# Issuing the second halves of the first six input tiles from ScalarE's DMA queue in a one-core hybrid decoder step

## The chip, the cores and the metric

One core of one Trainium2 chip runs the whole kernel. The metric is the device time of one execution in microseconds (us). Three runs of the kernel before gave 923.28, 923.93 and 924.47 us; their median is 923.93 us.

## What is computed

One layer of a decoder trunk over 1024 prompt rows and 8 sample rows (1032 rows, 1024 channels, float32). The start of it is what matters here:

```
h = rmsnorm(x, norm_g) * (1 + scale(c)) + shift(c)      # scale, shift, gate from silu(c) @ w_ada
p = h @ w_in                                            # twelve slices feed three branches
v = layernorm(gelu(p[b_v]))                             # the slice that is computed first
...                                                     # three branches, merge by sigmoid gates
x = x + gate(c) * (merged @ w_out);  y = rmsnorm(x, final_g)
```

The RMS norm needs the sum of squares over all 1024 channels of a row, so all of x has to be on the chip before any product of h can begin.

## The kernel before, in words

x lies transposed: eight tiles of 128 channels by 1032 rows. Each tile is loaded in two halves of 512 rows (256 KB each), x0 to x7 with halves a (`hf` 0) and b (`hf` 1); the eight sample columns come by a small DMA of their own (`xsm`, L342) and GpSimd copies them in (L156). The tiles go in the order 0, 4, 1, 5, 2, 6, 3, 7 (`ORDER`, L42).

Every engine works off its own list of instructions in the order of the program. SyncE (SP) issues all DMAs of the kernel before: `pk` (L105), `xsm` (L342), the sixteen halves of x (L155), and then by turns a tile of the v weights (`bvr`, L172) and two of the modulation weights (`ada`, L161). The framework gives every DMA one of eight completion counters in turn, in the order of the program; a DMA is issued only once the earlier one on its counter has landed. Counted from `pk`, the eighteenth DMA, x7b, so waits for the tenth, x5b.

ScalarE's list begins with a table load and a one-element activation (L127), the SiLU of the conditioning (L128, which waits for `pk`), a second table load and a one-element activation (L129). Then `sum_squares` (L189 to L206) follows: one Square per tile in the order of the tiles (L195, each waits for both halves of its tile), and for the last tile two Squares of half the width (L200). VectorE adds the squares up: five adds over whole tiles (L197) and four over halves (L203, L204). TensorE, which runs 110 dummy matmuls meanwhile (`warm_up`, L286, no input from x), forms the row sums from the added squares (L184). After it come the reciprocal root (L212 to L217), its spreading over the partitions (L226), the modulation product (`ada_mm`, L267) with its transposes (L275), the scaling of x (L241, L251), the split of h into two parts (L255, L259) and the first v products (L337 to L339). The rest of the kernel, over 800 us of it, is a row of matmul jobs that the change does not touch.

The order of the load around the change:

```
    Q.dma_start(xsm, ins["xT2"])
    for k in ORDER:
        load_x(k)
    for i in range(3):
        load_wbv(i)
        ada[i] = load_ada(ORDER[i])
    ss = sum_squares()
```

`Q` is SyncE, `A_` ScalarE, `G_` GpSimd, `V` VectorE.

Of the kernel before, what the change touches and what calls it, by code (L numbers as in the profile page):

```python
# [33 lines left out]
HP, HS = SEQ // 2, NS // 2  # L34
H = HP + HS
# [6 lines left out]
ORDER = (0, 4, 1, 5, 2, 6, 3, 7)  # L42
# [4 lines left out]
OC = ((128, 388, 4), (644, 388, 4), (0, 256, 2))  # L47
OE = 128
WIN = (2, 4, 8, 16)


def f32(ap):
# [4 lines left out]
def hybrid_step_kernel(ctx: ExitStack, tc: tile.TileContext, ins, outs):  # L57
# [8 lines left out]
    def S(name, cols=SLOT, dt=F32, rows=P):  # L66
        return sp.tile([rows, cols], dt, tag="T", name=name)
# [10 lines left out]
    def samples(ap):  # L78

        return halves(ap)[:, :, HP:H]  # L80
# [7 lines left out]
    V, A_, G_, PE, Q = nc.vector, nc.scalar, nc.gpsimd, nc.tensor, nc.sync  # L88
# [57 lines left out]
    xh = {}  # L146
# [5 lines left out]
    def load_x(k):  # L152
        xh[k] = S(f"x{k}", T)
        for hf in range(2):
            Q.dma_start(xh[k][:, H * hf : H * hf + HP], ins[f"xT{hf}"][:, k, :])  # L155
        G_.tensor_copy(samples(xh[k]), xsm[:, k, :].rearrange("p (h t) -> p h t", h=2))  # L156

    def load_ada(k):
# [184 lines left out]
    for k in ORDER:  # L343
        load_x(k)
# [34 lines left out]
    for i in range(KD):  # L379
        k = ORDER[i]  # L380
# [461 lines left out]
    def c_pair(g, n):  # L842
        st = {}
        w = WIN[g]

# [474 lines left out]
```

## Time and profile before

| | us |
|---|---|
| median of three runs | 923.93 |
| the profiled execution, device time | 925.24 |
| its span, first to last instruction | 923.5 |
| TensorE busy | 903.7 |
| ScalarE busy | 354.8 |
| VectorE busy | 563.0 |
| last half of x landed, first Square of the last tile | 17.48 |
| first row sum on TensorE | 18.99 |

The profile is one execution under the hardware profiler. The span is counted from the first to the last instruction, and 1.74 us of the device time lie outside it. Times in the rows are us from the span's start. An engine's name with a q behind it (SPq, ACTq) is that engine's sequencer, which issues DMAs and waits on semaphores. The granted clock is the share of TensorE's full clock: 1.00 is 2.4 GHz and 0.50 is 1.2 GHz.

### The profile page before, as it was taken

To read this page: it belongs to the slowest core of one execution; us is meant where nothing else is said; L and a number is where in the kernel's file an instruction comes from. 1 tells how busy PE (TensorE), PEld (TensorE's weight loads), DVE (VectorE), ACT (ScalarE), POOL (GpSimd) and SP (SyncE) were. 2 spreads that over 40 slices of the span, in tenths; PEclk is the share of its full clock that TensorE was granted. 3 is DMA by queue.
4 is the path that set the end of the run, shared out by engine and by line. 5 is a ranking of instruction groups with operands and counts; after the bars stand their busy time and mean duration, and the time that the engine had idled before them with its cause. 6 is when DMAs were issued, how large, how long until landed. Compare 5 with 4: busy or idle time off the path is not lost.

```text
span 923.5 us, 16546 instructions
## 1 busy us (share of the span) xinstructions
PE 903.7 (98%) x6910; PEld 874.1 (95%) x6910; DVE 563.0 (61%) x1016; ACT 354.8 (38%) x639; POOL 37.5 (4%) x76
## 2 busy tenths in 40 slices
PE   7998999999999999999999999999999999999995
PEld 7666999999999999999999999999999899999994
DVE  4686757656666576656465566574454466583634
ACT  5565473454342333335343454444422301431211
POOL 1354000000000000000000000000000000000001
PEclk8899999999999999999999999999999999999997
DMA  9904222212321212123304205132579834170103
GB/s 322 384 6 116 79 93 68 82 47 106 101 92 47 69 47 69 47 82 121 132 1 160 94 12 190 52 124 96 207 297 343 300 137 183 50 225 1 61 10 115
DMA packets 50058, 110.15 MB, mean 119 GB/s; under 512 B 10552, under 2 KB 21560, under 8 KB 49984
## 3 DMA queue, kind: packets, MB, share of 16 engines
q1 hardware_dynamic: 49984, 109.10, 34.0%
q8 instruction: 54, 0.88, 0.4%
q14 instruction: 20, 0.16, 0.1%
HBM read 85.24 MB, written 23.84 MB: 118 GB/s over the span
## 4 chain that ended last, share of the span: by engine, by line
PE 91%; POOL 2%; DVE 2%; DMA 1%; issue 1%; ACT 1%; SPq 0%; DVEq 0%; POOLq 0%; ACTq 0%
PE o L1077 3%; PE o L1078 3%; PE o L1079 3%; PE g_2B L525 2%; PE g_0B L525 2%; PE g_3B L528 2%; PE g_3B L525 2%; PE g_2B L527 2%; PE g_2B L528 2%; PE g_0B L527 2%; PE g_3B L527 2%; PE g_1B L528 2%; PE g_1B L525 2%; PE g_0B L528 2%; PE g_1B L527 2%; DMA x<-in_xT 1%
## 5 line engine op out<-in xcount | busy, mean ns | idle before, releaser
L1077 PE MATMUL o<-mh,woh 128*128 128x388 f32 (+1 forms) x192 | 62.2, 324 | 0.0
L1078 PE MATMUL o<-ml,woh 128*128 128x388 f32 (+1 forms) x192 | 61.4, 320 | 0.0
L1079 PE MATMUL o<-mh,wol 128*128 128x388 f32 (+1 forms) x192 | 61.3, 319 | 0.0
L1077 PEld LDWEIGHTS o<-mh,woh 128*128 128x128 f32 x192 | 36.1, 188 | 0.3
L1078 PEld LDWEIGHTS o<-ml,woh 128*128 128x128 f32 x192 | 36.1, 188 | 0.3
L1079 PEld LDWEIGHTS o<-mh,wol 128*128 128x128 f32 x192 | 36.1, 188 | 0.0
L1180 ACT ACTIVATE osq<-xr 128x388 f32<-128x388 f32 (+1 forms) x21 | 10.3, 491 | 48.4 <-DVE xr L1169 28.0
L337 PE MATMUL v<-bvw,hhi 128*128 128x512 f32 x64 | 27.2, 425 | 1.6 <-ACT v L613 1.1
L339 PE MATMUL v<-bvw,hlo 128*128 128x512 f32 x64 | 25.8, 403 | 1.1 <-DVE hlo L259 0.8
L91 ACT ACTIVATE mh<-acc 128x516 fp32r<-128x516 f32 (+1 forms) x14 | 9.2, 690 | 44.4 <-DVE acc L979 40.7
L338 PE MATMUL v<-bvw,hhi 128*128 128x512 f32 x64 | 25.5, 398 | 0.0
L1166 DVE SCALAR_TENSOR_TENSOR xr<-o,gt,xr 128x384 f32<-128x384 f32 x16 | 9.8, 614 | 18.5 <-PE o L1079 18.5
L525 PE MATMUL g_2B<-t,g_2w 128*128 128x258 f32 x72 | 20.4, 284 | 0.0
L528 PE MATMUL g_3B<-hhi,g_3wB 128*128 128x258 f32 x72 | 20.4, 283 | 0.0
L525 PE MATMUL g_0B<-t,g_0w 128*128 128x258 f32 x72 | 20.4, 283 | 0.0
L528 PE MATMUL g_1B<-hhi,g_1wB 128*128 128x258 f32 x72 | 20.4, 283 | 0.0
L337 PEld LDWEIGHTS v<-bvw,hhi 128*128 128x128 f32 x64 | 12.3, 192 | 8.6 <-issue 3.3
L528 PE MATMUL g_2B<-hhi,g_2wB 128*128 128x258 f32 x72 | 20.3, 283 | 0.0
L527 PE MATMUL g_0B<-hlo,g_0wB 128*128 128x258 f32 x72 | 20.3, 282 | 0.0
L527 PE MATMUL g_2B<-hlo,g_2wB 128*128 128x258 f32 x72 | 20.3, 282 | 0.0
L525 PE MATMUL g_3B<-t,g_3w 128*128 128x258 f32 x72 | 20.3, 282 | 0.0
L528 PE MATMUL g_1B<-t,g_1w 128*128 128x258 f32 x72 | 20.3, 282 | 0.0
(1043 smaller groups left out, 3490.7 us busy)
## 6 DMA issues: line engine op xcount, KB each, us to landing
sig<-sd SPq DMA_DIRECT2D x24, 516.0 KB, 5.9
ada<-in_ada SPq DMA_DIRECT2D x18, 512.0 KB, 8.6
yr<-yd SPq DMA_DIRECT2D x12, 516.0 KB, 10.2
x<-in_xT SPq DMA_DIRECT2D x16, 256.0 KB, 5.9
gr<-in_ada_g SPq DMA_DIRECT2D x8, 512.0 KB, 10.4
wor<-in_wo SPq DMA_DIRECT2D x8, 512.0 KB, 5.4
xr<-in_xf SPq DMA_DIRECT2D x8, 512.0 KB, 3.9
sd<-g_0o SPq DMA_DIRECT2D x6, 516.0 KB, 3.3
```

What stands on the lines that cost most here:

```text
L91: A_.activation(hi, src, AF.Copy)
L337: PE.matmul(vacc[i], lhsT=lh, rhs=w[:, 0, :], start=start, stop=False)
L338: PE.matmul(vacc[i], lhsT=lh, rhs=w[:, 1, :], start=False, stop=False)
L339: PE.matmul(vacc[i], lhsT=ll, rhs=w[:, 0, :], start=False, stop=stop)
L525: PE.matmul(o, lhsT=w[:, 0, f_], rhs=bh, start=start and k == 0, stop=False, skip_group_check=True)
L527: PE.matmul(o, lhsT=w[:, 0, f_], rhs=bl, start=False, stop=False, skip_group_check=True)
L528: PE.matmul(o, lhsT=w[:, 1, f_], rhs=bh, start=False, stop=stop and k == KW - 1, skip_group_check=True)
L1077: PE.matmul(o, lhsT=wo_h[k][:, w], rhs=cols(mhi[k]), start=start, stop=False)
L1078: PE.matmul(o, lhsT=wo_h[k][:, w], rhs=cols(mlo[k]), start=False, stop=False)
L1079: PE.matmul(o, lhsT=wo_l[k][:, w], rhs=cols(mhi[k]), start=False, stop=stop)
L1166: V.scalar_tensor_tensor(x[:, :m], ps[:, :m], gt[:, f, 0:1], x[:, :m], ALU.mult, ALU.add)
L1180: A_.activation(o_like(c, sq), x, AF.Square)
```

## The change

The half b of the tiles 0, 4, 1, 5, 2 and 6 is issued by ScalarE into its own DMA queue. The half a of these tiles, and both halves of tiles 3 and 7, stay with SyncE. Nothing else differs; the DMAs keep their order in the program, and so their completion counters.

```diff
+XQ = 6
...
     def load_x(k):
         xh[k] = S(f"x{k}", T)
         for hf in range(2):
-            Q.dma_start(xh[k][:, H * hf : H * hf + HP], ins[f"xT{hf}"][:, k, :])
+            q = A_ if hf and k in ORDER[:XQ] else Q
+            q.dma_start(xh[k][:, H * hf : H * hf + HP], ins[f"xT{hf}"][:, k, :])
         G_.tensor_copy(samples(xh[k]), xsm[:, k, :].rearrange("p (h t) -> p h t", h=2))
```

In the order of the program the DMAs are: pk, xsm, x0a, x0b*, x4a, x4b*, x1a, x1b*, x5a, x5b*, x2a, x2b*, x6a, x6b*, x3a, x3b, x7a, x7b, and then the weights; a star marks those that ScalarE issues now. In ScalarE's list the six stand behind the activation of L129 and ahead of the first Square.

## Rows read from the trace of the kernel before

**Rows 1.** The page's table of busy time: engine, us, share of the span, instructions.

```profile
PE 903.7 (98%) x6910; PEld 874.1 (95%) x6910; DVE 563.0 (61%) x1016; ACT 354.8 (38%) x639; POOL 37.5 (4%) x76
```

**Rows 2.** The chain that ended last, from the start to the first v products: start us, us, what held it.

```profile
1.72 0.42 SPq L155
...
4.56 0.43 SPq L155
...
5.04 6.39 DMA x<-in_xT
...
11.44 5.96 DMA x<-in_xT
...
17.48 0.64 ACT sq L200
...
18.15 0.71 DVE sq L204
...
18.99 3.65 PE ss L184 x24
22.64 1.86 PE pada L267 x16
```

**Rows 3.** The timeline of ScalarE from L128 to the last Square: start us, us, engine, line, operation, out<-in, count, and in brackets the idle time before it and what ended it.

```profile
2.75 0.27 ACT L128 ACTIVATE sc<-pk 128x72 f32<-128x72 f32 x1 [0.46 <-DMA pk<-in_pk]
3.04 1.28 ACT L129 ACT_TABLE_LOAD   x1
4.33 0.20 ACT L129 ACTIVATE warm<-ones 128x1 f32<-128x1 f32 x1
5.46 1.06 ACT L195 ACTIVATE sq<-x 128x1032 f32<-128x1032 f32 x1 [0.92 <-DMA x<-in_xT]
8.84 1.06 ACT L195 ACTIVATE sq<-x 128x1032 f32<-128x1032 f32 x1 [2.32 <-DMA x<-in_xT]
10.18 1.06 ACT L195 ACTIVATE sq<-x 128x1032 f32<-128x1032 f32 x1 [0.28 <-DMA x<-in_xT]
11.53 1.06 ACT L195 ACTIVATE sq<-x 128x1032 f32<-128x1032 f32 x1 [0.28 <-DMA x<-in_xT]
12.85 1.06 ACT L195 ACTIVATE sq<-x 128x1032 f32<-128x1032 f32 x1 [0.25 <-DMA x<-in_xT]
14.16 1.07 ACT L195 ACTIVATE sq<-x 128x1032 f32<-128x1032 f32 x1 [0.25 <-DMA x<-in_xT]
15.51 1.06 ACT L195 ACTIVATE sq<-x 128x1032 f32<-128x1032 f32 x1 [0.28 <-DMA x<-in_xT]
17.48 1.16 ACT L200 ACTIVATE sq<-x 128x516 f32<-128x516 f32 x2 [0.92 <-DMA x<-in_xT]
```

**Rows 4.** Busy time by stretch: us from the start, then the stretch's length, busy us (instructions) of PE, PEld, DVE, ACT and POOL, the granted clock, the mean busy share of the 16 DMA engines, and GB/s.

```profile
2.50:3.50 1.00, 1.00 (x7) 1.00 (x6) 0.17 (x1) 0.74 (x2) 0.30 (x3) 1.00 0.70 163
3.50:5.50 2.00, 2.00 (x14) 2.00 (x14) 0.00 (x0) 1.06 (x3) 0.76 (x7) 1.00 0.99 354
5.50:9.00 3.50, 3.50 (x34) 3.50 (x33) 0.00 (x0) 1.18 (x2) 0.00 (x0) 1.00 0.89 228
9.00:15.50 6.50, 6.41 (x58) 6.21 (x56) 5.13 (x5) 5.16 (x5) 0.00 (x0) 1.00 1.05 396
15.50:18.40 2.90, 0.00 (x0) 0.00 (x0) 1.98 (x3) 1.98 (x3) 0.00 (x0) 1.00 1.04 410
18.80:32.00 13.20, 13.01 (x70) 8.88 (x71) 8.56 (x25) 5.39 (x13) 1.66 (x6) 0.50 1.03 411
```

**Rows 5.** What ScalarE's sequencer carried out for L128: line, engine, operation, count, duration ns min/median/max, first and last start us.

```profile
L128 ACTq EVENT_SEMAPHORE  x1: 17/17/17, 2.7 to 2.7; - x1
```

**Rows 6.** A later stretch of ScalarE: its timeline, and ahead of it the one instruction that its sequencer carried out for L303 between 58.5 and 60 us (the columns as in rows 5 and 3).

```profile
L303 ACTq EVENT_SEMAPHORE  x1: 17/17/17, 59.0 to 59.0; - x1
...
58.83 1.07 ACT L255 ACTIVATE hhi<-x 128x1032 fp32r<-128x1032 f32 x1 [0.56 <-POOL x L253]
59.80 0.37 ACT L270 ACTIVATE adap<-pada 128x256 f32<-128x256 f32 x1
60.07 0.62 ACT L177 ACTIVATE bvw<-bvr 128x512 fp32r<-128x512 f32 x1
62.62 0.64 ACT L303 ACTIVATE t<-x 128x516 fp32r<-128x516 f32 x1 [1.93 <-POOL x L299]
```

**Rows 7.** DMAs by the stretch in which they were issued (3.1 to 3.5, 3.5 to 4.05, 12.1 to 12.2 and 13.3 to 14 us, in this order): out<-in, engine, operation, count, KB each, median us from issue to landing. The first is x4b, the second x1a and the tail of its neighbour, the third the first `bvr`, the fourth the second `ada`.

```profile
x<-in_xT SPq DMA_DIRECT2D x1, 256.0 KB, 5.6
x<-in_xT SPq DMA_DIRECT2D x2, 256.0 KB, 5.7
bvr<-in_wbv SPq DMA_DIRECT2D x1, 256.0 KB, 5.9
ada<-in_ada SPq DMA_DIRECT2D x1, 512.0 KB, 7.2
```

**Rows 8.** The timeline of SP's queue up to 17 us, columns as in rows 3.

```profile
1.72 10.05 SPq L155 DMA_DIRECT2D x<-in_xT  x16
12.11 0.33 SPq L172 DMA_DIRECT2D bvr<-in_wbv  x1
12.76 0.98 SPq L161 DMA_DIRECT2D ada<-in_ada  x2
14.07 0.33 SPq L172 DMA_DIRECT2D bvr<-in_wbv  x1
```

**Rows 9.** The timeline of VectorE up to the row sums, TensorE's first use of a modulation weight and ScalarE's first use of a v weight, columns as in rows 3.

```profile
9.93 6.60 DVE L197 TENSOR_TENSOR sq<-sq,sq 128x1032 f32<-128x1032 f32 x5 [7.08 <-ACT sq L195]
16.64 0.70 DVE L203 TENSOR_TENSOR sq<-sq,sq 128x516 f32<-128x516 f32 x1
18.15 0.70 DVE L204 TENSOR_TENSOR sq<-sq,sq 128x516 f32<-128x516 f32 x1 [0.82 <-ACT sq L200]
...
22.57 1.93 PE L267 MATMUL pada<-ada,sc 128*32 128x256 f32 x16
...
21.28 0.61 ACT L177 ACTIVATE bvw<-bvr 128x512 fp32r<-128x512 f32 x1
```

## The prediction, made before the changed kernel ran

> **What bounds the kernel now.** I began with the busy times [rows 1]: TensorE is busy 98% of the span, so the long middle cannot move by a change to loads, and only a stretch in which TensorE does nothing useful is open. I then followed the chain of waits from the start [rows 2]. Up to 17.48 us it is loads of x alone: SP issues them every 0.47 us, the chain goes over to a transfer at 5.04, from its landing to the issue at 11.44, and with that transfer to 17.40. From there ScalarE's last Squares, one VectorE add and the row sums on TensorE follow without slack. The reader is to see two things. The issue at 11.44 (x7b, the eighteenth DMA) hangs on the landing of the one issued at 5.04 (x5b, the tenth): that is the framework's counter, eight DMAs apart. And the chain is not held by issuing: 256 KB per 0.47 us would be 557 GB/s, while the DMA engines move 396 to 410 GB/s at a busy share of 1.05 from 9.00 on [rows 4]. So the start lasts as long as 4.2 MB of x take to arrive. What SP's time is worth is nothing by itself.
>
> ScalarE waits for x, not the other way: each Square takes 1.06 us, the tiles come about 1.33 us apart, and 0.25 to 0.28 us of idle lie ahead of each Square from the third on [rows 3]. That is the slack that the change uses up.
>
> **When ScalarE issues.** The six DMAs stand behind L129 in its list. The latest they can begin is 4.53, when that activation is over (4.33 + 0.20) [rows 3]. The earliest is 2.7: ScalarE's sequencer itself waits there for pk [rows 5]. Between the two I take the early end, about 2.8, because of a later row: at 59.0 the sequencer carried out the semaphore wait of L303, while L255 was running and L270 and L177, both ahead of L303, had not begun [rows 6]. So it goes on at least two operations ahead of its engine, and behind L128 there are just two, the table load and the activation of L129.
>
> What one issue costs ScalarE no row shows; on SP it is 0.43 us [rows 2], later 0.33 [rows 8]. I take 0.43 for each, 2.6 us for the six. The dearer part is the counters. The first three on ScalarE wait for nothing, x5b waits for xsm, but x2b waits for x0b, and x6b waits for x4b, both now issued by ScalarE. Seven Squares and the two halves of the eighth are queued behind x6b, and VectorE's adds and TensorE's row sums behind those. **The first Square therefore starts only when x4b has landed, plus 0.43 us**, where before it began at 5.46 with x0.
>
> **When x4b lands.** I count landings by position in the stream. Before, the second, fourth, sixth, eighth, tenth, twelfth, fourteenth and sixteenth half had landed at the Square that it released: 5.46, 8.84, 10.18, 11.53, 12.85, 14.16, 15.51, 17.48 [rows 3]. x4b, the fourth, landed at 3.14 + 5.6 = 8.74, and the fifth at about 3.61 + 5.7 = 9.3 [rows 2, 7]. The change does not add bytes, so I keep these times for the n-th half and ask only which half it is. The first transfer of x is issued at 1.72 and bytes come at 163 GB/s from 2.5 [rows 2, 4], so about 1.2 us after an issue; ScalarE's queue then takes part from about 4.0, when x0a is nearly there. How two queues share the engines no row shows. The bounds are that SP's halves all go first or that ScalarE's do; I take equal shares, the middle. Then the pairs are x4a with x0b (positions 2 and 3, 6 us), x1a with x4b (4 and 5, 9.3), x5a with x1b (10.8), x2a with x5b (12.1), x6a with x2b (13.4), x3a with x6b (14.8), then x3b, x7a and x7b alone, the last at 17.4 as before.
>
> **The sum.** x4b at 9.3, ScalarE free at 9.8. Back to back a Square costs about 0.97 us: 1.06 less an overlap of 0.1, which is what the two of L200 show, 1.16 us for two that the chain has at 0.64 [rows 2, 3]. The first five Squares are then limited by ScalarE; it is free for the sixth, x6, at 9.8 + 5 x 0.97 = 14.7, just as x6b lands (14.8), and the seventh ends at 14.8 + 0.97 + 1.06 = 16.8. x7b comes at 17.4 and releases the last two Squares at 17.48 as before: slack 0.6 us. On VectorE the fifth add (6.60 / 5 = 1.32 us with gaps) ends at about 17.2 and L203 at 17.9, both later than before, but L204 waits for the Square until 18.15 anyway [rows 9]: slack 0.25 us. So the two bounds meet just inside, and the row sums begin at 18.99 again. The stretch after them at half clock (0.50 until 32.0 [rows 4]) stays as it is, since the dummy matmuls before it wait for no data and the row sums do not move.
>
> What else moves: SP is rid of six issues, but x3b waits for x1b (10.8) and x7b for x5b (12.1), so x7b is issued 0.7 us later than 11.44; it still stands ahead of its turn in the stream (16.7). Behind it, the first bvr goes from 12.11 to about 12.5, the first ada waits for x2b, 13.4 instead of 12.76, and the second bvr for x6b, 14.8 instead of 14.07 [rows 8]. The bvr lands 5.9 us later, at 18.4, and is used at 21.28; the ada lands some 7.2 us later, about 20.6, and is used at 22.57 [rows 7, 9]. Both edits are hidden by two to three us; without that cover they would cost their 0.4 to 0.7. GpSimd's copies and TensorE's dummies touch none of this.
>
> Sum: 0. The profiled execution, 925.24 us, is 1.31 over the median; a shift of nothing leaves the median at **923.9**.
>
> **Rivals.** *The lock-out on ScalarE (slower).* Place: the issue of x6b. It decides once x4b lands after about 10.0, and with VectorE's smaller slack from 9.6. If ScalarE issues only at 4.53, its data start at about 5.7, x4b becomes the seventh half, 10.8, the Squares end at 10.8 + 0.43 + 6.8 = 18.0 instead of 17.4: +0.6, 924.5. If SP's backlog goes first, seven halves precede x0b, x4b is the ninth at about 12.2, and the last tile's Squares begin at 19.4 instead of 17.48: +1.9, 925.8. For it: the slack is 0.25 us. Against it: rows 6, and nothing prefers SP's queue.
>
> *The second queue fills the slow stretch (faster).* From 5.50 to 9.00 the engines move 228 GB/s at a share of 0.89, against 396 later [rows 4]. With eight transfers out, that stretch is not short of work in the queue. If packets that hang in one queue leave room for the other, up to 3.5 x (1 - 228/396) = 1.5 us come back: 922.4. If the row sums then begin so early that the clock does not fall, their 3.65 us, the 1.86 of the modulation product and the work after them up to 32 us, some 13 us on TensorE [rows 2, 4], would run at up to twice the speed, 6 us more: 916. Against it: a busy share of 0.89 means that the engines, not the queue, were the limit, and ScalarE would then end the Squares late unless x4b comes early too.
>
> The Trainium skill, "DMA: Bandwidth & Descriptors", section "Issuing engines are not separate DMA queues", speaks against this rival and against the change: transfers started by different engines run on the same sixteen DMA engines and interleave, and starting them from several saves issuing time alone. By that rule the time is 923.9, by the rival 922.4. The rows on the rate after 9.00 fit the rule; that two queues interleave no run here shows yet.
>
> *The change is inert:* it can't be, every half b of the six tiles has its new issuer; only that the counters force the old order is possible, and that is the forecast.
>
> **How the numbers follow.** About 0.2% (1.85 us) is what a measurement of this kernel can tell from no change. Forecast, within 0.6 us of 923.9: 0.55. Lock-out: 0.27, mostly between +0.6 and +1.5, a third of it at +1.9 or more (both bounds together). Slow stretch filled: 0.18, half of it under 1.5 us, and about half with the clock's part or an earlier start on top. That makes faster 0.10, within 0.80, slower 0.10. The range reaches from the filled stretch and a little (922.0) to SP's backlog going first (925.7), which leaves out the clock's part and the worst lock-outs, not quite 2 in 10.
>
> **What would show it.** Right: ScalarE's first Square near 9.8, the next ones back to back without the idle of 0.25, the last pair at 17.4 to 17.6, row sums at 19.0, and six DMA issues on ScalarE, the first near 2.8, the fifth and sixth held by landings. Wrong: a seventh Square that ends after 17.5 (lock-out); more than 300 GB/s between 5.5 and 9 (filled stretch); a granted clock of 1.00 after 18.8; or a first issue of ScalarE after 4.5.

## The result and the profile after

The changed kernel takes 932.17 us (median; before 923.85 in the same comparison): 8.3 us more, ratio 1.0089, 95% interval 1.0076 to 1.0101. The forecast was no change, 923.9, with a range up to 925.7, so it missed on the slow side, and by more than its worst rival.

The profiled execution of the changed kernel took 931.62 us, span 929.9. Its timeline, columns as in [rows 3]; line numbers are one or two higher than before, so L157 is the load of x, L197 and L202 the Squares, L199 the adds, L186 the row sums:

```profile
1.72 5.01 SPq L157 DMA_DIRECT2D x<-in_xT  x10
6.83 0.41 SPq L174 DMA_DIRECT2D bvr<-in_wbv  x1
8.66 2.71 SPq L163 DMA_DIRECT2D ada<-in_ada  x2
13.79 0.33 SPq L174 DMA_DIRECT2D bvr<-in_wbv  x1
...
4.42 0.20 ACT L130 ACTIVATE warm<-ones 128x1 f32<-128x1 f32 x1
7.86 6.76 ACTq L157 DMA_DIRECT2D x<-in_xT  x6
14.67 1.06 ACT L197 ACTIVATE sq<-x 128x1032 f32<-128x1032 f32 x1 [10.05 <-DMA x<-in_xT]
...
20.59 1.06 ACT L197 ACTIVATE sq<-x 128x1032 f32<-128x1032 f32 x1 [0.26 <-DMA x<-in_xT]
22.55 2.02 ACT L197 ACTIVATE sq<-x 128x1032 f32<-128x1032 f32 x2 [0.89 <-DMA x<-in_xT]
24.47 1.14 ACT L202 ACTIVATE sq<-x 128x516 f32<-128x516 f32 x2
...
17.05 1.23 DVE L199 TENSOR_TENSOR sq<-sq,sq 128x1032 f32<-128x1032 f32 x1 [14.10 <-ACT sq L197]
...
26.62 3.65 PE L186 MATMUL ss<-ones,sq 128*86 128x1 f32 x24 [10.52 <-DVE sq L206]
```

Read against [rows 3, 8, 9]: ScalarE was ready to issue at 4.6 (4.42 + 0.20), its first issue started at 7.86, and the six took until 14.62. The first Square began at 14.67 instead of 5.46. SP was through with x at 6.73 and put weights into the queue from 6.83 on, where before the first one followed at 12.11, behind all of x. The row sums began at 26.62 instead of 18.99, 7.63 us late. That is enough for the loss, but it is not a term that adds up to the digit: the two profiled executions lie 6.4 us apart (925.24 and 931.62), the medians 8.3, and at the last v product the lag was 6.97 us (92.27 and 99.24).

What ScalarE's issues cost is in the view of that line (count: shortest, median and longest duration in ns, first and last start), and what the DMA engines moved meanwhile is in the windows, columns as in [rows 4]:

```profile
L157 SPq DMA_DIRECT2D x<-in_xT x10: 424/432/737, 1.7 to 6.0; - x10
L157 ACTq DMA_DIRECT2D x<-in_xT x6: 334/335/381, 7.9 to 14.3; - x6
```
```profile
5.50:9.00 3.50, 3.50 (x30) 3.50 (x29) 0.00 (x0) 0.00 (x0) 0.00 (x0) 1.00 0.94 267
9.00:15.50 6.50, 6.50 (x61) 6.50 (x60) 0.00 (x0) 0.83 (x1) 0.00 (x0) 1.00 1.06 407
...
18.80:32.00 13.20, 5.38 (x40) 4.19 (x40) 10.14 (x20) 6.44 (x10) 0.00 (x0) 0.54 1.03 409
```

Six issues of 0.34 us are 2 us out of 6.76: the rest is waiting. The engines were as busy as before (407 GB/s from 9 to 15.5), only with other bytes.

The waits are those of the completion counters. They were not dealt in the order of the text. The framework dealt them in an order of its own, merged from the two issuers' lists, in which ScalarE's DMAs come behind SP's whole run of x. The DMAs in that order, with the one whose counter each waits for (a star marks ScalarE's):

```
pk  xsm  x0a  x4a  x1a  x5a  x2a  x6a        no wait
x3a (pk)   x3b (xsm)   x7a (x0a)   x7b (x4a)
bvr (x1a)  x0b* (x5a)  ada (x2a)   x4b* (x6a)
x1b* (x3a) ada (x3b)   x5b* (x7a)  x2b* (x7b)
bvr (bvr)  x6b* (x0b)  ada (ada)   ada (x4b)
```

The trace bears it out: x5a's last piece landed at 7.84, x0b was issued at 7.86. Likewise x4b was issued at 9.74, after x6a's landing at 9.72, and x6b at 14.29, after x0b's at 14.27. x6b itself landed at 22.46; before, the last half of x, x7b, had landed at 17.40.

### The profile page after: what moved, and what is told of

Its sections match the earlier page's. It is cut to its first block, busy times and chain, and to the rows that moved or that the text cites. A ratio compares the mean times of both kernels' runs of the same rounds, so it can differ in the third digit from the quotient of the medians.

```text
span 929.9 us, 16542 instructions
## 1 busy us (share of the span) xinstructions
PE 901.5 (97%) x6910; PEld 873.1 (94%) x6910; DVE 562.8 (61%) x1016; ACT 354.4 (38%) x639; POOL 37.2 (4%) x76
## 4 chain that ended last, share of the span: by engine, by line
PE 89%; DMA 4%; POOL 2%; DVE 2%; issue 1%; ACT 1%; SPq 0%; DVEq 0%; POOLq 0%; ACTq 0%
PE o L1079 3%; PE o L1080 3%; PE o L1081 3%; DMA ada<-in_ada 3%; PE g_2B L527 2%; PE g_0B L527 2%; PE g_2B L529 2%; PE g_3B L527 2%; PE g_3B L529 2%; PE g_0B L529 2%; PE g_1B L530 2%; PE g_2B L530 2%; PE g_3B L530 2%; PE g_1B L527 2%; PE g_0B L530 2%; PE g_1B L529 2%
## 5 line engine op out<-in xcount | busy, mean ns | idle before, releaser
L530 PE MATMUL g_3B<-hhi,g_3wB 128*128 128x258 f32 x72 | 20.4, 283 | 0.0
L527 PE MATMUL g_3B<-hhi,g_3wB 128*128 128x258 f32 x72 | 20.3, 283 | 0.0
L529 PE MATMUL g_3B<-hlo,g_3wB 128*128 128x258 f32 x72 | 20.3, 282 | 0.0
```

The lines of the kernel that those rows point to most:

```text
L527: PE.matmul(o, lhsT=w[:, 0, f_], rhs=bh, start=start and k == 0, stop=False, skip_group_check=True)
L529: PE.matmul(o, lhsT=w[:, 0, f_], rhs=bl, start=False, stop=False, skip_group_check=True)
L530: PE.matmul(o, lhsT=w[:, 1, f_], rhs=bh, start=False, stop=stop and k == KW - 1, skip_group_check=True)
```

## The experiments

Theory 1: the order of the counters makes the loss. It has two effects, that the first tiles' Squares start late and that weights overtake x. Theory 2: two queues disturb each other whatever the order. Theory 3: the issues in ScalarE's list hold up the Squares. Later runs ask whether a second queue can help at all. The table gives for every kernel the median, three starts in its one profiled execution (us; the first whole-tile add on VectorE, the last pair of Squares on ScalarE, the row sums on TensorE) and the rate from 5.5 to 9 us. Line numbers shift by a few from kernel to kernel: `sq<-x` on ACT is a Square, `sq<-sq,sq` on DVE an add, `ss` on PE the row sums.

| kernel | median us | first add | last Squares | row sums | GB/s |
|---|---|---|---|---|---|
| before | 923.85 | 9.93 | 17.48 | 18.99 | 228 |
| after | 932.17 | 17.05 | 24.47 | 26.62 | 267 |
| one queue, order of after | 932.11 | 18.00 | 23.45 | 26.34 | 228 |
| x0b alone | 930.23 | 16.41 | 21.05 | 24.75 | 280 |
| weights held back | 930.12 | 16.52 | 21.16 | 24.86 | 196 |
| six, at the head | 925.36 | 11.43 | 16.07 | 19.77 | 367 |
| none, at the head | 924.07 | 9.82 | 18.21 | 19.72 | 279 |
| six from GpSimd | 925.28 | 12.13 | 17.53 | 20.50 | 242 |
| three, at the head | 923.88 | 9.64 | 16.18 | 17.98 | 371 |
| three, x0a first | 923.86 | 10.42 | 18.07 | 19.58 | 343 |
| none, x0a first | 925.02 | 9.99 | 17.52 | 19.02 | 218 |
| pk and three | 920.03 | 7.77 | 14.51 | 16.11 | 392 |
| pk and two | 920.25 | 7.73 | 15.26 | 16.77 | 361 |
| pk alone | 923.97 | 9.41 | 16.29 | 17.80 | 275 |

**One queue, order of after.** All DMAs go back to SP, but in the merged order listed above, so with the same counters; ScalarE issues nothing.

```diff
...
-    for i in range(3):
-        load_wbv(i)
-        ada[i] = load_ada(ORDER[i])
+    load_wbv(0)
+    half_x(0, 1)
+    ada[0] = [S3(f"ada0_{h}", 4, 256) for h in range(2)]
+    Q.dma_start(ada[0][0], ins["ada"][0, :, 0:4, :])
+    half_x(4, 1)
+    half_x(1, 1)
...
```

> All DMAs on SP's one queue, but in the order and with the counters that the changed kernel had (x0a, x4a, x1a, x5a, x2a, x6a, x3a, x3b, x7a, x7b, the first v weight, x0b, ada, x4b, x1b, ada, x5b, x2b, v weight, x6b and so on). ScalarE issues nothing. Theory 1: the order alone makes the loss; x6b lands at about 22.5, row sums begin at about 26.6, time 930 to 932. Theory 2 (two queues) and theory 3 (issues in ScalarE's list): neither is there, so most of the loss is gone, 924 to 926.

Measured 932.11, ratio to before 1.0089 (1.0073 to 1.0105), the loss of the change within 0.1 us. Its timeline:

```profile
14.88 1.06 ACT L199 ACTIVATE sq<-x 128x1032 f32<-128x1032 f32 x1 [10.28 <-DMA x<-in_xT]
16.91 2.02 ACT L199 ACTIVATE sq<-x 128x1032 f32<-128x1032 f32 x2 [0.96 <-DMA x<-in_xT]
...
18.00 6.59 DVE L201 TENSOR_TENSOR sq<-sq,sq 128x1032 f32<-128x1032 f32 x5 [15.08 <-ACT sq L199]
...
26.34 3.65 PE L188 MATMUL ss<-ones,sq 128*86 128x1 f32 x24 [11.04 <-DVE sq L208]
```

The reader is to see the same late first Square (14.88) and the same late row sums without any second queue. This shows that the order is enough for the whole loss; theories 2 and 3 are not needed. That the medians agree so closely is in part chance: the first add came 0.95 us later here (18.00) and the last Squares 1.02 us earlier (23.45).

**x0b alone on ScalarE** splits the loss: nothing overtakes, only the first tile is late.

```diff
-XQ = 6
+XQ = 1
```

> Only x0b goes to ScalarE (XQ = 1). Its counter is then that of x1a, so it is issued once x1a has landed, at about 8, still ahead of all weights. Theory 1: no overtaking; x0b lands at about 14, the first Square waits for it, and eight tiles of Squares back to back (7 x 0.97 + 1.16 = 7.95) end at about 22 instead of 18.64: 2 to 3.3 us on the start, time 925.5 to 927. Theory 2 (loss in proportion to what ScalarE's queue carries): 8.3 / 6 = 1.4 us, 925.2, with the fifteen other halves landing late. Theory 3 (issue time on ScalarE): 924.2 at most, one issue of 0.35 us.

Measured 930.23, 1.0069 (1.0054 to 1.0083): 6.4 us for a single half, against 1.6 to 3.1 expected.

```profile
8.38 0.39 ACTq L157 DMA_DIRECT2D x<-in_xT  x1
14.36 6.78 ACT L197 ACTIVATE sq<-x 128x1032 f32<-128x1032 f32 x7 [9.85 <-DMA x<-in_xT]
...
16.41 6.59 DVE L199 TENSOR_TENSOR sq<-sq,sq 128x1032 f32<-128x1032 f32 x5 [13.58 <-ACT sq L197]
...
24.75 3.65 PE L186 MATMUL ss<-ones,sq 128*86 128x1 f32 x24 [9.57 <-DVE sq L206]
```

The issue and the landing came where theory 1 put them (8.38, first Square 14.36), the price did not. I had priced the chain by ScalarE, seven Squares at 0.97. Behind it VectorE's adds take 1.32 each, 6.59 for five, and four half adds follow. In every kernel here in which the adds, whole and half, run without a gap, the row sums begin 8.34 to 8.37 after the first add (16.41 + 8.34 = 24.75). **The second bound of the start is therefore first add + 8.34**, beside the one by arrival, last Squares + 1.51 (17.48 + 1.51 = 18.99). Of the fourteen kernels of the table all but after begin the row sums within 0.1 us of the later of the two. In after the adds have gaps, since its Squares waited for x again, for 0.94 us at 17.95 and for 0.89 us at 22.55.

**Weights held back:** the changed kernel, with a one-element activation into the first v weight's buffer behind ScalarE's six issues.

```diff
     def load_wbv(i):
...
+        if i == 0:
+            A_.activation(bv["pair"][:, 0, 0:1], ones[:, 0:1], AF.Copy)
```

> The changed kernel, and a one-element activation on ScalarE behind its six issues that writes into the first v weight's buffer, so that SP issues no weight before x6b is issued: the weights can't overtake x any more, while the six halves b still come behind SP's ten. Theory 1: the loss has two parts, 5.1 us of overtaking (x6b landed at 22.46 instead of 17.40) and 2.6 us of Squares of three tiles behind it (row sums 26.62 - 18.99 = 7.63 in all). Here only the second is left: x6b lands at about 17.5, row sums at 21 to 22, time 925.5 to 927. Theory 2: x6b lands late again, over 20, time 929 to 932. Theory 3: as the changed kernel, 931 to 932.

Measured 930.12, 1.0066 (1.0051 to 1.0080): 2.0 us better than the change, where 5 to 7 were expected. SP's first weight went at 14.01, and the six issues ran from 6.16 to 13.24.

```profile
6.16 7.08 ACTq L157 DMA_DIRECT2D x<-in_xT  x6
...
13.70 1.06 ACT L199 ACTIVATE sq<-x 128x1032 f32<-128x1032 f32 x1 [0.21 <-DMA x<-in_xT]
15.43 5.83 ACT L199 ACTIVATE sq<-x 128x1032 f32<-128x1032 f32 x6 [0.66 <-DMA x<-in_xT]
...
16.52 6.59 DVE L201 TENSOR_TENSOR sq<-sq,sq 128x1032 f32<-128x1032 f32 x5 [13.70 <-ACT sq L199]
...
24.86 3.65 PE L188 MATMUL ss<-ones,sq 128*86 128x1 f32 x24 [8.42 <-DVE sq L208]
```

The direction held, the split did not: with no weight ahead of x the row sums are at 16.52 + 8.34 = 24.86, still set by the late first adds. The time lies in the range that the expectation gave theory 2 (929 to 932), but theory 2's sign, x6b after 20, is not there: x6b landed at 17.81, about where theory 1 had it. With the weights behind, the counters also fall otherwise: x0b waits for x1a here (landed at 6.14), as in the run before. The two runs measure the same part, the late first tile, and agree within 0.1 us (6.4 and 6.3 over before); the 2.0 that are left of the 8.3 are put down to the weights that overtake.

**Six, at the head.** The loads of x move to the head of the program and so of ScalarE's list. The counters then alternate between the two queues (x0b, pk, xsm, x0a, x4b, x4a and so on), nearly the order that the prediction had assumed (x5b waits for x0b, x2b for xsm, x6b for x4b).

```diff
+    xh = {}
+    xsm = cp.tile([P, KD, NS], F32, name="xsm")
+    Q.dma_start(xsm, ins["xT2"])
+    for k in ORDER:
+        xh[k] = S(f"x{k}", T)
+        for hf in range(2):
+            q = A_ if hf and k in ORDER[:XQ] else Q
+            q.dma_start(xh[k][:, H * hf : H * hf + HP], ins[f"xT{hf}"][:, k, :])
     ones = cp.tile([P, P], F32, name="ones")
...
```

> All loads of x stand at the head of the program, and so at the head of ScalarE's list too, with the same split (six halves b on ScalarE). Then the eight completion counters alternate between the two queues (x0b, x0a, x4b, x4a and so on), the weights come behind all of x, and two queues still work at once. Theory 1 (it is the place in the dealing of the counters: with the change ScalarE's halves got counters behind SP's whole run of x, were issued from 7.86 us on, and 2 MB of weights overtook x6b): x6b lands by about 16, x7b last at about 17.4, row sums at 18.5 to 19.2, time 923 to 924.5. Theory 2 (two queues disturb each other, or ScalarE's is served worse, whatever the order): x6b lands after 20 again and the time stays at 928 or more. Theory 3 (the Squares are locked out behind the issues in ScalarE's list): the issues are done early, the first Square starts once x0 is there, 924.

Measured 925.36, 1.0015 (1.0006 to 1.0024): 6.8 of the 8.3 us are gone, and 1.5 stay, where theory 1 had 923 to 924.5.

```profile
0.78 5.50 ACTq L119 DMA_DIRECT2D x<-in_xT  x6
6.32 1.28 ACT L136 ACT_TABLE_LOAD   x1 [6.32 <-DMA xsm<-in_xT]
...
9.40 6.77 ACT L199 ACTIVATE sq<-x 128x1032 f32<-128x1032 f32 x7
...
11.43 6.59 DVE L201 TENSOR_TENSOR sq<-sq,sq 128x1032 f32<-128x1032 f32 x5 [6.82 <-ACT sq L199]
...
19.77 3.62 PE L188 MATMUL ss<-ones,sq 128*86 128x1 f32 x24 [3.73 <-DVE sq L208]
```

Theory 2 falls here too: x6b landed at 11.36. What is left fits theory 3, in a small form: the issues end at 6.28, both table loads stand behind them, the first Square starts at 9.40 and the adds set the row sums. All of x had landed by 15.18, 2.2 us earlier than before, and nothing came of it. That raised a question, since from 5.5 to 9 us the engines moved 367 GB/s.

**None, at the head** (XQ = 0) is the control for the moved block.

> The loads of x at the head of the program as in the run before with six halves on ScalarE (which ran at 925.36 us, moved 367 GB/s from 5.5 to 9 us and had x7b landed at 15.2), but all sixteen on SP's queue. It is the control for that move. If a second queue that takes part from the start is what raised the rate: 228 GB/s or so from 5.5 to 9 as in the kernel before, x7b at 17.4, row sums at 19.0, 923.9 us. If the place in the program raised it: over 300 GB/s, x7b at 15 to 16, row sums at 17, 922 or less.

Measured 924.07, 1.0001 (0.9986 to 1.0016), at 279 GB/s, between the two rates expected. The moved block alone changes no time. In this execution x7b landed at 18.13, later than expected.

**Six from GpSimd:** the changed kernel with another queue, which has counters of its own.

```diff
-            q = A_ if hf and k in ORDER[:XQ] else Q
+            q = G_ if hf and k in ORDER[:XQ] else Q
```

> The changed kernel with the six halves b on GpSimd's queue instead of ScalarE's, at the same place in the program. Transfers of that queue have counters of their own, so they wait for nothing that SP has under way, and SP's ten halves still share eight counters. Theory 1 (the loss is the wait on counters behind SP's run of x): the six are issued from about 2 on, the first Square starts at 5.5 to 8, row sums at 18 to 19.5 (first Square + 10.4 or last landing + 1.6, the later), 923 to 925 us. A rival: it is the place in the list or a second queue as such; then x0b lands at 12 to 14, row sums after 24, 929 us or more. A further cost that no run has shown is what GpSimd needs for one issue; it would show as landings of the halves b more than 1.2 us apart.

Measured 925.28, 1.0014 (1.0005 to 1.0024), just over the expected 923 to 925. The same six halves at the same place in the program lose 1.2 us instead of 8.3 when they don't share SP's counters. An issue takes GpSimd 0.54 us, the first at 2.12, the last at 5.91. But x4 was complete only at 11.04 (the second Square), the first add came at 12.13 and the row sums at 12.13 + 8.37; the rate stayed at 242 GB/s.

**Three, at the head** (XQ = 3 in the version with six), **three, x0a first** (there pk and xsm come behind x0a and x0b), and **none, x0a first** (the same on SP alone):

```diff
-XQ = 6
+XQ = 3
...
-    Q.dma_start(pk, ins["pk"])
...
-    Q.dma_start(xsm, ins["xT2"])
...
+            if not hf and k == ORDER[0]:
+                Q.dma_start(pk, ins["pk"])
+        if k == ORDER[0]:
+            Q.dma_start(xsm, ins["xT2"])
```

The first two lines are the whole edit of the first; the second has all of them, the third too with XQ = 0.

> The same with three halves on ScalarE (x0b, x4b, x1b), which are among the first eight DMAs and so wait for no counter. ScalarE is through with its issues at about 2.1 and with both table loads at about 5.1, so the first Square starts at about 5.5 and not at 9.4. If two queues from the start raise the rate: x7b at 15.2 to 15.8, row sums 16.8 to 17.5, 922.0 us (1.6 to 2.2 less than before, times a half to one), and as low as 916 if the row sums come before the granted clock falls at about 18.4. If the second queue gives nothing: 923.9. If a queue on ScalarE disturbs its own work: 924.5 or more.

> As the one with three halves, but SP begins with x0a, and the small loads pk and xsm come behind x0a and x0b. SP's first half of x is then issued at 0.8 instead of 1.7. If the start is bound by bytes from the first issue on, this gives 0.3 to 0.8 us on top of the three halves: x7b at 14.6 to 15.2, row sums at 16.3 to 16.9. If the small loads' delay (SiLU and the sample columns come later) matters: the first Square after 6 and nothing gained.

> The same order with x0a first, all on SP's queue: whether the earlier first byte alone makes the gain. If the second queue is what counts: 230 to 280 GB/s from 5.5 to 9, x7b at 16.5 to 17.4, row sums 18 to 19, 923 to 924 us. If the early start is what counts: as with the three halves on ScalarE, x7b at about 15, 922 or less.

Measured 923.88 (ratio 0.9996, 0.9982 to 1.0010), 923.86 (0.9994, 0.9979 to 1.0008) and 925.02 (1.0008, 0.9996 to 1.0021): no gain. The first two missed the 922 that had been hoped for, and the third came 1 us over its 923 to 924, at 218 GB/s instead of 230 to 280. The first Square of the version with three, and under it that of three with x0a first:

```profile
7.59 4.93 ACT L199 ACTIVATE sq<-x 128x1032 f32<-128x1032 f32 x5 [1.09 <-DMA x<-in_xT]
...
8.37 4.88 ACT L201 ACTIVATE sq<-x 128x1032 f32<-128x1032 f32 x5 [0.93 <-POOL x L162]
```

In the version with three, x0b went ahead of pk in time, and pk landed at 4.62 instead of about 2.7, so ScalarE was through with the SiLU and the second table load only at 6.49. It then waited another 1.09 us for x0a, which SP had issued at 1.72, behind pk and xsm, and which landed at 7.48. The row sums came at 9.64 + 8.34 = 17.98. With x0a first, xsm came late instead (landed at 8.10), and GpSimd's copy of the sample columns released the first Square at 8.37. So once x is early the small loads count, by their own landing or by the half of x that they delay. That the row sums of the version with three came 1.0 us earlier in its profiled execution and its median did not move is not explained here; the runs of before beside it lay between 920.6 and 926.5.

**Pk and three; pk and two; pk alone.** ScalarE issues pk first, and then three halves, two or none; SP begins with xsm and x0a. The rest is as in the versions at the head.

```diff
-    Q.dma_start(pk, ins["pk"])
+    A_.dma_start(pk, ins["pk"])
```

> Loads of x at the head, and ScalarE issues pk first and then x0b, x4b, x1b; SP begins with xsm and x0a. Row sums have begun at the later of first Square + 10.39 and last landing + 1.59 in every run so far. With pk landed by 2.6 and x0 by 5.5, the first Square starts at 5.7 to 6.5 (before 5.46; 7.59 with pk behind x0b), so the first bound gives 16.1 to 16.9; x7b at 15.4 to 16.1 gives 17.0 to 17.7. Row sums at 17 to 17.7, 1.3 to 2 us ahead of before, time 922 to 922.7. If two queues from the start do not raise the rate between 5.5 and 9 us after all: x7b at 17.4, 923.9.

> As the one with pk and three halves on ScalarE, with two (x0b, x4b). ScalarE is free 0.45 us earlier. If the arrival of the last half bounds it, the same or up to 0.5 us later than with three; if the first Square bounds it, up to 0.45 us earlier. 922 to 923.5.

> The control for the version with pk and three halves on ScalarE, which ran at 920.03 us: only pk is left on ScalarE, all sixteen halves of x are on SP again, with the same counters. If the halves on the second queue make the gain (392 GB/s from 5.5 to 9 us there, 218 to 279 wherever SP's queue alone carried x): 220 to 280 GB/s, x7b at 16.9 to 17.6, row sums 18.5 to 19.2, 923.4 to 924.1 us. If SP's earlier start by one issue (0.47 us) or the moved pk makes it: row sums before 18, 922.5 us or less.

Measured with three 920.03, ratio **0.9961** (0.9949 to 0.9974), with two 920.25, 0.9962 (0.9948 to 0.9976), with none 923.97, 0.9996 (0.9985 to 1.0007). The first two beat the kernel before by 3.8 to 4.0 us, more than was expected of either. First the version with three, timeline and windows, and then the same of the one with pk alone:

```profile
0.79 0.40 ACTq L106 DMA_DIRECT2D pk<-in_pk  x1
1.22 1.41 ACTq L119 DMA_DIRECT2D x<-in_xT  x3
...
5.74 2.00 ACT L199 ACTIVATE sq<-x 128x1032 f32<-128x1032 f32 x2
...
14.51 1.16 ACT L204 ACTIVATE sq<-x 128x516 f32<-128x516 f32 x2 [0.24 <-DMA x<-in_xT]
...
16.11 1.05 PE L188 MATMUL ss<-ones,sq 128*86 128x1 f32 x12 [0.38 <-DVE sq L208]
17.51 1.05 PE L188 MATMUL ss<-ones,sq 128*86 128x1 f32 x12 [0.36 <-DVE rm0x L216]
```
```profile
3.50:5.50 2.00, 2.00 (x11) 2.00 (x11) 0.00 (x0) 1.97 (x4) 0.54 (x5) 1.00 1.03 377
5.50:9.00 3.50, 3.50 (x34) 3.50 (x33) 1.23 (x1) 3.25 (x5) 0.00 (x0) 1.00 1.05 392
...
18.80:32.00 13.20, 13.18 (x78) 7.58 (x70) 9.62 (x23) 7.22 (x14) 3.49 (x9) 0.74 1.03 412
```
```profile
16.29 1.16 ACT L204 ACTIVATE sq<-x 128x516 f32<-128x516 f32 x2 [0.22 <-DMA x<-in_xT]
...
17.80 1.05 PE L188 MATMUL ss<-ones,sq 128*86 128x1 f32 x12 [1.61 <-DVE sq L208]
```
```profile
3.50:5.50 2.00, 2.00 (x11) 2.00 (x11) 0.00 (x0) 1.37 (x3) 0.44 (x4) 1.00 0.92 311
5.50:9.00 3.50, 3.50 (x30) 3.50 (x29) 0.00 (x0) 1.39 (x2) 0.00 (x0) 1.00 0.89 275
...
18.80:32.00 13.20, 11.94 (x87) 7.20 (x87) 9.68 (x29) 6.93 (x15) 1.84 (x8) 0.87 1.03 411
```

Both bounds now meet: first add 7.77 + 8.34 = 16.11, and the last Squares at 14.51 + 1.51 = 16.02, three us earlier than before. ScalarE is through with its issues at 2.63, none of which waits for a counter, and the first Square starts at 5.74, 0.28 later than before. (The rule in the expectation, first Square + 10.39, had not held in every run: in the one queue with the order of after it gives 25.27, and the row sums began at 26.34, because the second tile's Square waited too. First add + 8.34 holds there.)

The three halves on ScalarE are the only edit between the two kernels. They raise the rate from 275 to 392 GB/s and bring 3.9 us by the medians, 3.2 by the ratios, and the two intervals lie apart. That they make the gain is shown; the way from the start to the end is not. The control's time and rate are those expected if the halves make the gain, but its row sums began at 17.80, before the 18 that was named as the sign of the other case: 1.2 us earlier than before, and its median gained nothing, as in the version with three at the head (1.0 earlier). And the lead of the version with three over the control was 1.69 us at the row sums, 0.65 at the first v product (26.08 and 26.73), and 3.90 at the last one (86.66 and 90.56): most of it opened among the v products, which no run here takes apart. So it is not shown that the 2.9 us by which the row sums begin earlier than in the kernel before make 2.9 of the 4.0. The granted clock does not decide it either: over 18.8 to 32 us it was 0.74 with three, 0.87 with pk alone and 0.50 before, and the first twelve matmuls of the row sums took 1.05 us in the first two (before, all 24 took 3.65).

## Why the prediction was wrong

- *The start lasts as long as x takes to arrive.* Right for the kernel before: its row sums follow the last Squares by 1.51, as do those of the three controls on SP alone (1.50 to 1.51). Incomplete: the bound by the adds, 9.93 + 8.34 = 18.27, lay only 0.72 us below.
- *The counters are dealt in the order of the program, so that x2b waits for x0b and x6b for x4b.* **This step failed, and with it the forecast.** [rows 2] showed the eight counters on one issuing engine, where the order of the text and the dealt order are the same; I carried that over to two engines and stated it as a fact in the description of the change. The runs showed in its place that x0b waits for x5a, x4b for x6a and x6b for x0b: ScalarE's first issue came at 7.86 instead of 2.8, and the first Square at 14.67 instead of 9.8. The order alone on one queue gives 932.11.
- *ScalarE issues from about 2.8.* Not tested: in after the counter held it until 7.86, past the 4.5 that was named as a sign of being wrong. On the reading of [rows 5, 6] nothing can be said.
- *0.43 us for one issue on ScalarE.* Too dear, it was 0.34, and of no weight.
- *Equal shares of the two queues, the n-th half lands as before.* Never came to it in after. Where both queues work from the start, the halves land earlier.
- *Squares back to back at 0.97, slack 0.6; VectorE's slack 0.25.* The Squares are right (6.78 for seven). VectorE's term was mis-sized in the working itself: it let the fifth add follow the sixth Square at once, to 17.2, but five adds of 1.32 in a row behind Squares of 0.97 fall behind. With the first Square at 9.8, the first add comes 2.03 later (as 9.40 and 11.43 with six at the head), at 11.83, and the row sums at 11.83 + 8.34 = 20.17, not 18.99. The version with six at the head comes near that case, though its Squares are late for another reason, the table loads behind the issues: 9.40, 19.77, and 925.36 us. So even with the order that I had assumed the row sums would, by this estimate, have begun 1.2 us late (with six at the head they were 0.8 late, and the median 1.5 higher).
- *The weights are hidden.* The wrong question: I asked whether they would come too late. They came too early, at 6.83 instead of 12.5, and ahead of x. That is the smaller part, the 2.0 us that are left.
- *The lock-out on ScalarE* had the right sign and the right engine, ScalarE with its Squares queued behind issues that wait. Its place, x6b, and its price, up to 1.9, came from the wrong order; the wait that decides was x0b's, at the head of the six.
- *The second queue fills the slow stretch* was wrong for the change (267 GB/s), but the rate is higher where ScalarE's queue takes part from the start (392 against 275 GB/s). The Trainium skill, "DMA: Bandwidth & Descriptors", section "Issuing engines are not separate DMA queues", says that starting transfers from several engines saves issuing time alone. That pair does not decide it: the eighth DMA was issued at 2.21 us with three halves on ScalarE and at 3.62 with pk alone, 1.41 sooner, and the row sums came 1.69 sooner, so that most of this lead can be saved issuing time. No run separates that from what a second queue does by itself.

## What to carry to other kernels

When DMAs move to another engine's queue, look up in the built program which earlier DMA each now waits for: the counters are shared between the queues and dealt in an order that the framework makes from both engines' lists, so that the first byte needed can end up behind the last. In the two kernels that gained, the halves that moved were among the first eight DMAs and stood ahead of everything slow in their engine's list, and the small load on which that engine's first work hangs went ahead of them. Price a late start through every engine of the chain behind it; here the adds on VectorE, not the Squares that I had watched, set 6.4 us for one late half.

## What had not been expected of the hardware

With SP alone carrying x, the engines moved 218 to 279 GB/s from 5.5 to 9 us in all five kernels of that kind, in one profiled execution each. With ScalarE's queue taking part from 0.8 to 1.2 us on (five kernels) it was 343 to 392. GpSimd's queue from 2.1 on (242) and ScalarE's from 6.2 to 8.4 on (196 to 280) did not raise it. Why an early second queue does, and whether it is the queue or the earlier issue of the first eight DMAs, no run shows.
